# S5 matmuls on four 64x64 quadrants, the direct kernel's operand read in line, and the cell norm ahead of the output-gate blocks

## The chip, the core and the metric

The kernel runs on one core of a Trainium2 chip. The metric is the device time of one execution in microseconds (us). The engines are named as the profile names them: PE (TensorE's matmuls; PEld its weight loads), DVE (VectorE), ACT (ScalarE), POOL (GpSimd) and SP (SyncE, which issues most DMA transfers). Each engine works through its own list of instructions in order, and they meet through semaphores only.

## What is computed

One encoder layer on 272 positions (16 meta tokens and 256 inputs) of width 2048, in fp32:

```
z = RMSNorm(h) @ w_in                      # 2048 -> u_s5 1024 | qk 1024 | v 1024 | o 1024 | gates 32
y_s5: 64 groups of 16 channels, 64 complex states each, forward and backward:
    s[t] = lam * s[t-1] + Bbar u[t];  y = Re(C s) + d * u
    gelu, then y * sigmoid(y @ w_glu + b_glu), then RMSNorm
y_ml: mLSTM with 8 heads, forward and backward, num / max(|den|, exp(-m)), summed over both directions
    RMSNorm over each head's 128 values (the cell norm), times sigmoid(o)
h = h + [y_s5 || y_ml] @ w_out
h = h + (silu(conv(RMSNorm(h) @ w_gate)) * (RMSNorm(h) @ w_up)) @ w_down
out = RMSNorm(h)[16:]
```

## The kernel before, in words

Everything is held transposed: channels on the 128 partitions, positions along the free axis. `win_block(b)` (L455) makes one 128-row block of z: 16 matmuls of 128x128 weights (two records each in the trace, as every fp32 matmul), into a PSUM bank of the ring "mm". Block 0 is the gates, 1 to 8 are u, 9 to 16 q and k, 17 to 24 v, 25 to 32 o.

The S5 part cuts time into C = 68 chunks of T = 4 positions. A pair j of groups (32 pairs) has its first group on partitions 0 to 63 and its second on 64 to 127; m = 0 to 7 takes four pairs. The steps:

- `s5_tables` (L322) makes powers of lam from `par`, and `td`, a copy of some of them in DRAM.
- `in_coefs(m)` (L518) loads those (tcf) and builds the input coefficients on DVE (L529 to L532, ring of two). `in_proj(m)` (L535) multiplies them with U, the chunked input: per pair one bank of the ring "s5", eight 64x64 matmuls (L545), of which the first group uses rows and columns 0 to 63 of the array and the second rows and columns 64 to 127. ACT copies the bank to ST (L546).
- `rec_local`, `rec_carry`, `rec_spread` (L549 to L583) run the recurrence over chunks on DVE, in two halves of four m.
- `s5_coefs(m)` (L809) loads bc (512 KB, ring of two), builds zx and c1 on DVE (L822 to L832), and makes the direct kernel kp, the response within a chunk: per pair eight matmuls (L839) of 64 rows and 32 columns, each reading c1 as "k h", a stride of four elements, into the one bank "acc". Then come 32 matmuls mo (L856) of c1 with the states, into a bank of "s5". DVE adds d to the middle tap in PSUM (L863) and ACT copies kp to gx (L867, one buffer for two m). After each odd m, ACT issues four DMAs (L873) that spread gx into ms.
- `s5_out(b)` (L879), for the two m of b, is called after the s5_coefs that follows: POOL reorders ms to m0 (L881), PE adds m0 times U to the banks of mo (L887), ACT copies (L889), and two DMAs bring the result through `yd` back into U (L890, L891).
- `s5_gelu` (L898), later `s5_glu` (L908), which streams w_glu.

The mLSTM part: `gate_rows`, `qk_block`, `v_block`, `ml_meta`, then `ml_head(h)` for eight heads, with `den` kept in a bank "acc" over all of them and nb_ in "ml". `o_block(h)` makes the output gates. `ml_norm` (L764), a generator, takes 1/den, brings it through DRAM (rd) to all partitions as rb, scales num (L777 on DVE, L778 on POOL), squares it (L780), sums it on PE (L781), takes the root, and brings that through rsd to rsb for the products of L792 to L796. It runs after s5_glu. The products with w_out follow: first with the S5 half (L1030 on), where DVE multiplies each PSUM bank with R5 (t, L1042) and POOL adds it to h1, then with the mLSTM half (L1052 on). The MLP streams the rest.

Weights of mm3 and mm2 are split on the fly: `piece` loads raw (SP), ACT rounds to hi (L239), DVE makes lo (L240).

What sets the order: the code gives a program order and some pieces a high priority (`hp`). A planner of the framework (`schedule_with_timeline_sim=True`, L1149) then simulates the engines with its own costs, and puts on each engine what is ready in its simulation, by priority; that order is fixed in the program. `behind(a, b)` (L270) keeps a after b on one engine, without a wait. A ring's tile waits until the tile before it in the same buffer has been read. PSUM has eight banks: mm 2, s5 4, ml 1, acc 1 (L182).

## Time and profile before

| | |
|---|---|
| three runs | 1301.99 us median, 1300.67 to 1307.05 |
| profiled execution | 1304.81 us, its span 1303.0 us |
| mean granted TensorE clock | 0.983 |
| busy | PE 1238.1 us (95%), DVE 790.7 (61%), ACT 539.2 (41%), POOL 214.9 (16%) |
| chain that ended last, by engine | PE 76%, DVE 12%, DMA 7% |
| L466 (block matmuls), PE | 254.1 us |
| L266 and L267 (MLP), PE | 251.6 + 244.1 + 198.5 + 197.9 us |

The span is the time from the first to the last instruction of the profiled execution, and all stretches are in us from its start. A row of instructions gives engine, line, operation, output<-inputs and shape, and xcount; "idle before" is how long the engine stood before it, and the arrow names what ended that. The share of busy time is a mean over stages that have different limits; it says little about a single one.

### The profile page before, as it was taken

How to read it: one execution, taken by the hardware profiler on the slowest of the kernel's cores; microseconds unless marked ns; L12 is line 12 of the kernel's file. 1: busy time of each engine (PE TensorE's matmuls, PEld its weight loads, DVE VectorE, ACT ScalarE, POOL GpSimd, SP SyncE). 2: the span in 40 equal slices, each digit the busy share in tenths (PEclk: the TensorE clock that was granted, in tenths of full speed). 3: DMA queues.
4: the chain of work that ended last, by engine and by line, in shares of the span. 5: the costliest groups of instructions: out<-in, count | busy, mean ns of one | idle time of the engine just before them, and what ended most of it. 6: DMA issues, size and time to landing. Idle time of an engine off the chain costs nothing.

```text
span 1303.0 us, 21967 instructions
## 1 busy us (share of the span) xinstructions
PE 1238.1 (95%) x8865; PEld 1114.3 (86%) x8865; DVE 790.7 (61%) x1097; ACT 539.2 (41%) x858; POOL 214.9 (16%) x314
## 2 busy tenths in 40 slices
PE   6888998899999989999999999999999999999995
PEld 4777787778889879999999999888999999998885
DVE  4659998410114788766666665555666666665554
ACT  3522121232344545554444444333444444445552
POOL 1300000011210363221111111000111111120101
PEclk9989999999999999999999999999999999999998
DMA  9596433344325565555555556666555555556663
GB/s 340 146 274 188 149 130 107 93 148 146 109 62 177 168 208 164 181 187 182 186 183 183 188 183 180 192 192 190 187 188 182 187 184 182 189 173 194 188 193 113
DMA packets 88762, 227.79 MB, mean 175 GB/s; under 512 B 20604, under 2 KB 36436, under 8 KB 88660
## 3 DMA queue, kind: packets, MB, share of 16 engines
q1 hardware_dynamic: 81652, 223.95, 54.6%
q10 hardware_dynamic: 7008, 2.43, 0.7%
q8 instruction: 70, 1.15, 0.4%
q14 instruction: 32, 0.26, 0.1%
HBM read 219.81 MB, written 5.48 MB: 173 GB/s over the span
## 4 chain that ended last, share of the span: by engine, by line
PE 76%; DVE 12%; DMA 7%; issue 2%; ACT 1%; POOL 1%; ACTq 0%; SPq 0%; DVEq 0%; POOLq 0%
PE ps_mm L266 25%; PE ps_mm L267 13%; PE ps_mm L466 8%; PE ps_mm L255 8%; PE ps_mm L256 8%; PE ps_mm L257 8%; DMA bc<-bcs 1%; DVE ST L555 1%; DVE t L554 1%; DVE t L553 1%; DMA X<-xt 1%; DMA raw<-wglu 1%; DMA ms<-gx 1%; DVE ST L556 1%; DVE X L952 1%
## 5 line engine op out<-in xcount | busy, mean ns | idle before, releaser
L240 DVE TENSOR_TENSOR lo<-raw,hi 128x1024 fp32r<-128x1024 f32 (+1 forms) x312 | 392.9, 1259 | 256.7 <-ACT hi L239 230.2
L239 ACT ACTIVATE hi<-raw 128x1024 fp32r<-128x1024 f32 (+1 forms) x312 | 324.0, 1038 | 398.9 <-PE ps_mm L266 161.0
L466 PE MATMUL ps_mm<-X,wf 128*128 128x272 f32 (+1 forms) x1056 | 254.1, 400 | 19.1 <-DVE X L302 12.7
L466 PEld LDWEIGHTS ps_mm<-X,wf 128*128 128x128 f32 x1056 | 204.6, 196 | 61.3 <-DVE X L302 14.3
L266 PE MATMUL ps_mm<-X,hi 128*128 128x512 f32 x704 | 251.6, 398 | 0.0
L266 PE MATMUL ps_mm<-a,hi 128*128 128x512 f32 x704 | 244.1, 390 | 0.0
L256 PE MATMUL ps_mm<-X,hi 128*128 128x258 f32 x704 | 200.3, 284 | 0.0
L255 PE MATMUL ps_mm<-X,hi 128*128 128x258 f32 x704 | 198.9, 283 | 0.0
L267 PE MATMUL ps_mm<-a,lo 128*128 128x256 f32 x704 | 198.5, 282 | 0.0
L267 PE MATMUL ps_mm<-X,lo 128*128 128x256 f32 x704 | 197.9, 281 | 0.0
L257 PE MATMUL ps_mm<-X,lo 128*128 128x258 f32 x704 | 197.6, 281 | 0.0
L266 PEld LDWEIGHTS ps_mm<-X,hi 128*128 128x128 f32 x704 | 132.2, 188 | 30.2
L266 PEld LDWEIGHTS ps_mm<-a,hi 128*128 128x128 f32 x704 | 132.1, 188 | 27.7
L1094 POOL TENSOR_TENSOR gt<-gt,R 128x256 f32<-128x256 f32 x44 | 59.6, 1355 | 488.7 <-ACT gt L1093 488.7
L257 PEld LDWEIGHTS ps_mm<-X,lo 128*128 128x128 f32 x704 | 134.5, 191 | 0.0
L255 PEld LDWEIGHTS ps_mm<-X,hi 128*128 128x128 f32 x704 | 132.4, 188 | 1.9
L267 PEld LDWEIGHTS ps_mm<-X,lo 128*128 128x128 f32 x704 | 134.0, 190 | 0.0
L267 PEld LDWEIGHTS ps_mm<-a,lo 128*128 128x128 f32 x704 | 133.1, 189 | 0.0
L256 PEld LDWEIGHTS ps_mm<-X,hi 128*128 128x128 f32 x704 | 132.8, 189 | 0.0
L742 DVE SCALAR_TENSOR_TENSOR w<-ps_s,w 128x256 f32<-128x256 f32 (+3 forms) x32 | 10.2, 354 | 64.1 <-PE ps_s L730 42.1
L1099 DVE TENSOR_TENSOR u<-ps_mm,gt 128x512 f32<-128x512 f32 x44 | 30.4, 691 | 29.3 <-PE ps_mm L267 28.1
L255 PE MATMUL ps_mm<-y,hi 128*128 128x258 f32 x128 | 36.6, 288 | 6.5 <-DVE t L1042 5.9
(317 smaller groups left out, 1460.2 us busy)
## 6 DMA issues: line engine op xcount, KB each, us to landing
raw<-wg SPq DMA_DIRECT2D x88, 512.0 KB, 3.9
raw<-wu SPq DMA_DIRECT2D x88, 512.0 KB, 4.0
wf<-win SPq DMA_DIRECT2D x65, 512.0 KB, 4.0
raw<-wd SPq DMA_DIRECT2D x64, 512.0 KB, 3.6
raw<-wout SPq DMA_DIRECT2D x32, 512.0 KB, 4.1
raw<-wd SPq DMA_DIRECT2D x32, 384.0 KB, 3.8
tcf<-td SPq DMA_DIRECT2D x16, 256.0 KB, 7.1
bc<-bcs SPq DMA_DIRECT2D x8, 512.0 KB, 3.5
```

What stands on the lines that cost most here:

```text
L239: S.activation(hi[:, a:b], raw[:, a:b], AF.Copy)
L240: V.tensor_tensor(out=lo[:, a:b], in0=raw[:, a:b], in1=hi.bitcast(F32)[:, a:b], op=ALU.subtract)
L255: nc.tensor.matmul(out_ap, h, xh, start=(first and i == 0), stop=False)
L256: nc.tensor.matmul(out_ap, h, xl, start=False, stop=False)
L257: nc.tensor.matmul(out_ap, l, xh, start=False, stop=(last and i == n - 1))
L266: nc.tensor.matmul(both[:, :, :cols], h, x, start=(i == 0), stop=False)
L267: nc.tensor.matmul(both[:, 1, :cols], l, x[:, 0, :], start=False, stop=(i == n - 1))
L466: nc.tensor.matmul(p[:, :L - t0], w[k // 8][:, k % 8 * P:k % 8 * P + P], X[:, k, t0:], start=(k == 0), stop=(k == KD - 1))
L553: V.tensor_tensor(out=t1, in0=src, in1=lr[:, sl].unsqueeze(2).unsqueeze(3).to_broadcast([P, 32, 2, n]), op=ALU.mult)
L554: V.tensor_tensor(out=t2, in0=src[:, :, ::-1, :], in1=li[:, sl, :].unsqueeze(3).to_broadcast([P, 32, 2, n]), op=ALU.mult)
L1094: G.tensor_tensor(out=t, in0=t, in1=R2[:, 2:], op=ALU.mult)
L1099: V.tensor_tensor(out=u, in0=p.rearrange("p (j t) -> p j t", j=2), in1=t.unsqueeze(1).to_broadcast([P, 2, SEQ]), op=ALU.mult)
```

## The change

The inputs are laid out so that of every odd pair the two groups change places in the S5 parameters (`swapped` in `prepare`); U stays as it is. Matmuls of an even and an odd pair then take all four 64x64 quadrants in turn, into two banks (`rows_of(g ^ o)`). kp's columns lie as (h, k), so that c1 is read in line and the output goes in runs of four. kp takes two banks of "acc", which has two now; "ml" is gone and its users take "acc". The mo banks of an even and an odd pair serve two m. ACT copies kp before DVE adds d, in gx. POOL's copy in s5_out waits for the last mo of its two m. `par` is loaded behind the second X chunk instead of the last. ml_norm's first part (1/den) is emitted ahead of the o_blocks, its head loop behind them but ahead of s5_glu, its sums on PE behind the last o_block matmul; the rest stays behind s5_glu.

```diff
+    def swapped(a, ga, ja):
+        a = np.moveaxis(a, (ga, ja), (0, 1)).copy()
+        a[:, 1::2] = a[::-1, 1::2]
+        return np.moveaxis(a, (0, 1), (ga, ja))
+
     for i, a in enumerate((are, aim, ldt)):
         r = a.reshape(2, NP, 2, 64)
-        par[:, i, :64] = r.transpose(2, 3, 1, 0).reshape(P, 64)
+
+        par[:, i, :64] = swapped(r, 2, 1).transpose(2, 3, 1, 0).reshape(P, 64)
...
     def bank(tag):
-        return ps.tile([P, 512], F32, tag=tag, name="ps_" + tag, bufs={"mm": 2, "s5": 4, "ml": 1, "acc": 1}[tag])
+        return ps.tile([P, 512], F32, tag=tag, name="ps_" + tag, bufs={"mm": 2, "s5": 4, "acc": 2}[tag])
 
...
             behind(xd, last_raw[0])
             x_scale(q, a)
             if q == 1:
+                pd = nc.sync.dma_start(par, A["par"])
+                behind(pd, xd)
                 pieces.append(whole(w0[:, 1024:]))
-                behind(last_raw[0], xd)
-        pd = nc.sync.dma_start(par, A["par"])
-        behind(pd, xd)
+                behind(last_raw[0], pd)
+        pd = xd
     behind(nc.sync.dma_start(cst, A["cst"][:, :NC0]), pd)
     bts = [STf[:, 64 * C + 1024 * i:64 * C + 1024 * i + 1024] for i in range(4)]
...
+    def rows_of(g):
+        return slice(64 * g, 64 * g + 64)
...
     def in_proj(m, ic):
-        for q in range(4):
-            j = 4 * m + q
-            p = bank("s5")
-            pv = p[:, :4 * C - 4].rearrange("p (d r c) -> p d r c", d=2, r=2)
+        for q0 in (0, 2):
+            pv = [bank("s5")[:, :4 * C - 4].rearrange("p (d r c) -> p d r c", d=2, r=2) for _ in range(2)]
             for d in range(2):
-                uj = U[:, j, 0:C - 1] if d == 0 else U[:, j, UW - C + 1:][:, ::-1]
                 for ri in range(2):
-                    for g in range(2):
-                        gg = slice(64 * g, 64 * g + 64)
-                        nc.tensor.matmul(pv[gg, d, ri, :], ic[gg, q, d, ri, :], uj[gg], start=True, stop=True)
-            S.copy(ST[:, 2 * j:2 * j + 2, :, 1:], pv)
+                    for o in range(2):
+                        j = 4 * m + q0 + o
+                        uj = U[:, j, 0:C - 1] if d == 0 else U[:, j, UW - C + 1:][:, ::-1]
+                        for g in range(2):
+                            nc.tensor.matmul(pv[o][rows_of(g ^ o), d, ri, :], ic[rows_of(g), q0 + o, d, ri, :], uj[rows_of(g)],
+                                             start=True, stop=True)
+            for o in range(2):
+                j = 4 * m + q0 + o
+                S.copy(ST[:, 2 * j:2 * j + 2, :, 1:], pv[o])
 
...
         rd = dr.tile([40, N], F32, name="rd")
         nc.sync.dma_start(rd, rec)
         dump("rec", rec)
+        yield
...
-            nc.tensor.matmul(ss[:40, :N], er_(h), sq, start=(h == 0), stop=(h == 7))
+            behind(nc.tensor.matmul(ss[:40, :N], er_(h), sq, start=(h == 0), stop=(h == 7)), last_o[0])
             yield
...
+    pos = [None, None]
+    mo0, mo1 = {}, {}
+    gxs = [None]
+
     def s5_coefs(m, tb):
-        kp = bank("acc")
-        po = bank("s5")
-        mo0 = [None, None]
+        kp = [bank("acc"), bank("acc")]
+        if m % 2 == 0:
+            pos[:] = [bank("s5"), bank("s5")]
+            mo0.clear()
...
+        for i in range(2):
             for n_, (dd, ri) in enumerate(((1, 0), (1, 1), (0, 0), (0, 1))):
...
+                c0 = 0 if dd == 1 else 3
+                for o in range(2):
+                    w = (2 * (2 * i + o) + dd) * 2 + ri
+                    for g in range(2):
+                        gg = rows_of(g ^ o)
+                        mk_ = nc.tensor.matmul(
+                            kp[o][32 * g:32 * g + 32, 112 * i:112 * i + 112].rearrange("p (h k) -> p h k", k=7)[:, :, c0:c0 + 4],
+                            zx[gg, w].rearrange("p h e -> p (h e)"), c1[gg, w],
+                            start=(n_ == 0), stop=(n_ == 3), skip_group_check=True)
+                        if mkp is not None:
+                            behind(mk_, mkp)
+                        mkp = mk_
+        for i in range(2):
             for dd in range(2):
                 for ri in range(2):
...
+                    for o in range(2):
+                        j = 4 * m + 2 * i + o
+                        x = ST[:, 2 * j + dd, ri, 0:C]
+                        x = x if dd == 0 else x[:, ::-1]
+                        w = (2 * (2 * i + o) + dd) * 2 + ri
+                        cc_ = (2 * (m % 2) + i) * C
+                        for g in range(2):
+                            gg = rows_of(g ^ o)
+                            mo = nc.tensor.matmul(pos[o][rows_of(g), cc_:cc_ + C], c1[gg, w].rearrange("p h k -> p (h k)"), x[gg],
+                                                  start=((o, g) not in mo0), stop=False, skip_group_check=True)
+                            mo1[o] = mo
+                            if (o, g) not in mo0:
+                                mo0[o, g] = mo
+                            else:
+                                behind(mo, mo0[o, g])
         if m % 2 == 0:
             gxs[0] = gxr("gx", [P, 2, 4, 7, 16])[:64]
         gx = gxs[0]
...
+        for o in range(2):
+            S.copy(gx[:, m % 2, o::2], kp[o][:64, :224].rearrange("p (i h k) -> p i k h", i=2, k=7))
+        V.tensor_tensor(out=gx[:, m % 2, :, 3, :], in0=gx[:, m % 2, :, 3, :], in1=ed[:, 4 * m:4 * m + 4, :], op=ALU.add)
         if m % 2 == 0:
...
+            return None
 
         ms = m0r("ms", [P, 8, T, 16])
         for s in range(T):
             nc.scalar.dma_start(ms[s:P:T].rearrange("p e k h -> p e (k h)"),
                                 gx[0:64:2, :, :, 3 - s:7 - s].rearrange("p m q k h -> p (m q) (k h)"))
...
+        return ms
+
+    def s5_out(b, pos, ms, fence):
+        first = None
         m0 = m0r("m0", [P, 8, 16, T])
...
+        mc = G.tensor_copy(m0, ms.rearrange("p e k h -> p e h k"))
+
+        tc.add_manual_dep(mc.ins, fence.ins.name, mybir.DependencyInfo(
+            mybir.DependencyClass.Sync, mybir.DependencyReason.DATA), reason="bank")
         ysc = ysr("ysc", [P, 4, 2, C])
...
+        for i in range(2):
             for q in range(4):
+                cc_ = (2 * i + q // 2) * C
                 for g in range(2):
...
+                    gg = rows_of(g)
+                    mm_ = nc.tensor.matmul(pos[q % 2][gg, cc_:cc_ + C], m0[gg, 4 * i + q].rearrange("p h k -> p (h k)"),
+                                           U[gg, 8 * b + 4 * i + q, U0:U0 + C], start=False, stop=(i == 1 and q > 1), skip_group_check=True)
+                    if first is None:
+                        first = mm_
+                    else:
+                        behind(mm_, first)
+        for o in range(2):
+            S.copy(ysc[:, o::2].rearrange("p q m c -> p m q c"), pos[o][:, :4 * C].rearrange("p (m q c) -> p m q c", m=2, q=2))
         nc.scalar.dma_start(yd[b].rearrange("q x t m c -> (x t) q (m c)"), ysc.rearrange("p q m c -> p q (m c)"))
         nc.sync.dma_start(U[:, 8 * b:8 * b + 8, U0:U0 + C], yd[b].rearrange("q x t m c -> (q x) (t m) c"))
 
...
         ml_head(h)
+    nrm = ml_norm()
+    next(nrm)
     for h in range(8):
         o_block(h)
+    for h in range(8):
+        next(nrm)
     h1 = hx.tile([P, KD, N], F32, tag="h1", name="h1")
     o_gates()
     s5_glu()
-    for _ in ml_norm():
+    for _ in nrm:
         pass
```

## Rows read from the trace of the kernel before

**Rows 1.** busy us by stretch: length, PE, PEld, DVE, ACT, POOL, PEclk, DMA, GB/s

```profile
92.00:204.00 112.00, 102.03 (x716) 86.11 (x712) 108.73 (x209) 24.43 (x62) 1.08 (x15) 0.98 0.48 151
204.00:264.00 60.00, 51.07 (x1122) 47.82 (x1122) 33.73 (x46) 9.89 (x20) 4.63 (x3) 0.94 0.36 102
264.00:380.00 116.00, 114.14 (x579) 94.01 (x576) 14.60 (x42) 41.34 (x107) 21.38 (x43) 0.99 0.38 119
380.00:404.00 24.00, 24.00 (x116) 20.89 (x114) 2.45 (x2) 3.51 (x6) 0.00 (x0) 1.00 0.27 88
436.00:500.00 64.00, 54.76 (x400) 49.27 (x400) 49.07 (x61) 26.29 (x39) 36.93 (x32) 0.97 0.59 182
```

**Rows 2.** lines of PE, 204 to 273; behind the bar busy us, mean ns, idle

```profile
L839 PE MATMUL ps_acc<-c,zx 64*32 64x64 f32 x512 | 31.2, 291 | 6.8 <-DVE c L832 3.6 <-ACT gx L867 3.1
L856 PE MATMUL ps_s<-ST,c 64*64 64x68 f32 x512 | 16.9, 221 | 0.0
```

**Rows 3.** groups by line, PE, 60 to 130, the in-projection

```profile
L545 PE MATMUL ps_s<-U,ic 64*64 64x67 f32 x512 | 19.8, 242 | 8.0 <-DMA U<-ud 3.8 <-ACT ST L546 1.9 <-DVE ic L531 1.9
```

**Rows 4.** chain of waits, 204 to 275; start us, us, what

```profile
212.14 3.38 DMA bc<-bcs
...
227.84 4.87 DMA bc<-bcs
...
234.74 0.60 ACTq L873
...
241.15 1.84 POOL m L881
...
251.78 0.59 ACTq L873
...
264.70 0.04 ACT U L904
...
271.25 1.05 PE ps_s L887 x28
```

**Rows 5.** timeline of DVE, 90 to 275; start, us, instruction, count, idle, releaser

```profile
91.93 1.22 DVE L529 TENSOR_TENSOR ic<-tcf,ST 128x1024 f32<-128x1024 f32 x1 [1.73 <-PE ps_s L545]
...
210.89 1.23 DVE L830 TENSOR_TENSOR c<-bc,la 128x1024 f32<-128x1024 f32 x1 [0.44 <-PE ps_s L856]
...
240.86 1.23 DVE L831 TENSOR_TENSOR c<-bc,lb 128x1024 f32<-128x1024 f32 x1 [2.99 <-DMA bc<-bcs]
...
248.12 0.23 DVE L863 TENSOR_TENSOR ps_acc<-ps_acc,ed 64x64 f32<-64x64 f32 x1 [1.40 <-PE ps_acc L839]
...
250.09 1.22 DVE L830 TENSOR_TENSOR c<-bc,la 128x1024 f32<-128x1024 f32 x1 [1.16 <-PE ps_s L856]
...
251.35 1.22 DVE L832 TENSOR_TENSOR c<-c,c 128x1024 f32<-128x1024 f32 x1
```

**Rows 6.** timeline of PE, 196 to 276; the middle row from a window cut at 244.15

```profile
204.16 0.89 PE L839 MATMUL ps_acc<-c,zx 64*32 64x64 f32 x12 [3.61 <-DVE c L832]
...
244.13 0.28 PE L839 MATMUL ps_acc<-c,zx 64*32 64x64 f32 x2
...
264.08 5.31 PE L466 MATMUL ps_mm<-X,wf 128*128 128x272 f32 x22
```

**Rows 7.** groups by line, DVE, 436 to 500

```profile
L777 DVE TENSOR_TENSOR num<-num,rb 128x516 f32<-128x516 f32 x8 | 6.6, 830 | 5.2 <-DMA rb<-rd 5.2
L792 DVE TENSOR_TENSOR rsb<-num,rsb 128x258 f32<-128x258 f32 x8 | 5.6, 723 | 2.5 <-DMA rsb<-rsd 2.5
```

**Rows 8.** who waited for whom, PE, 436 to 500; total us, times, longest

```profile
PE ps_mm L255 <- DVE t L1042: 7.8, 5, 2.2
```

**Rows 9.** timeline of DVE, 0 to 40, one row

```profile
19.27 1.17 DVE L302 TENSOR_SCALAR X<-X,vec 128x272 f32<-128x272 f32 x4 [2.79 <-ACT sqx L300]
```

**Rows 10.** DMA packets, 8 to 22, while the inputs load

```profile
DMA packets 1658, 5.42 MB, mean 387 GB/s; under 512 B 184, under 2 KB 324, under 8 KB 1658
```

**Rows 11.** timeline of ACT, 196 to 276, the first ms issues

```profile
217.49 2.61 ACTq L873 DMA_DIRECT2D ms<-gx  x4
```

More of the change, by code (lines that the diff above doesn't have):

```diff
@@ L465, in win_block @@
         for k in range(KD):
-            nc.tensor.matmul(p[:, :L - t0], w[k // 8][:, k % 8 * P:k % 8 * P + P], X[:, k, t0:],
-                             start=(k == 0), stop=(k == KD - 1))
+            last_o[0] = nc.tensor.matmul(p[:, :L - t0], w[k // 8][:, k % 8 * P:k % 8 * P + P], X[:, k, t0:],
+                                         start=(k == 0), stop=(k == KD - 1))
         return p
@@ L620, in gate_rows @@
         for i in range(2):
-            pc = bank("ml")
+            pc = bank("acc")
             nc.tensor.matmul(pc[:, :40], c[:, META + 128 * i:META + 128 * i + 128], ident[:, :40], start=True, stop=True)
@@ L663, in v_block @@
             S.copy(vm[:, h, :], vt[:, 0:META])
-            pv = bank("ml")
+            pv = bank("acc")
             for i, src in enumerate((vt[:, 16:144], vt[:, 144:272])):
@@ L668, in v_block @@
             if h == 7:
-                pv = bank("ml")
+                pv = bank("acc")
                 nc.tensor.transpose(pv[:, :P], vm.rearrange("p h s -> p (h s)"), ident)
@@ L694, in ml_meta @@
             G.tensor_copy(kv[:, h // 2, h, :], (kE if h % 2 == 0 else kO)[:, h // 2, 0:16])
-        sm = bank("ml")
+        sm = bank("acc")
         for j in range(4):
@@ L745, in ml_head @@
         G.tensor_tensor(out=sm[:, 128:], in0=ab, in1=bb[:, 0:130], op=ALU.add)
-        nf, nb_ = bank("s5"), bank("ml")
+        nf, nb_ = bank("s5"), bank("acc")
         mmu = nc.tensor.matmul
@@ L832, in s5_coefs @@
         V.tensor_tensor(out=c1, in0=c1, in1=c2, op=ALU.add)
-        for qq in range(4):
+        for i in range(2):
             for n_, (dd, ri) in enumerate(((1, 0), (1, 1), (0, 0), (0, 1))):
-                c0 = 0 if dd == 1 else 48
-                w = (2 * qq + dd) * 2 + ri
-                for g in range(2):
-                    gg = slice(64 * g, 64 * g + 64)
-                    mk_ = nc.tensor.matmul(
-                        kp[32 * g:32 * g + 32, 112 * qq + c0:112 * qq + c0 + 64],
-                        zx[gg, w].rearrange("p h e -> p (h e)"),
-                        c1[gg, w].rearrange("p h k -> p k h"),
-                        start=(n_ == 0), stop=(n_ == 3), skip_group_check=True)
-                    if mkp is not None:
-                        behind(mk_, mkp)
-                    mkp = mk_
@@ L847, in s5_coefs @@
-        for qq in range(4):
-            j = 4 * m + qq
+                c0 = 0 if dd == 1 else 3
[10 more added lines that the diff above has]
+                        mkp = mk_
@@ L849, in s5_coefs @@
+        for i in range(2):
             for dd in range(2):
                 for ri in range(2):
-                    x = ST[:, 2 * j + dd, ri, 0:C]
-                    x = x if dd == 0 else x[:, ::-1]
-                    w = (2 * qq + dd) * 2 + ri
-                    for g in range(2):
-                        gg = slice(64 * g, 64 * g + 64)
-                        mo = nc.tensor.matmul(po[gg, qq * C:qq * C + C], c1[gg, w].rearrange("p h k -> p (h k)"), x[gg],
-                                              start=(mo0[g] is None), stop=False, skip_group_check=True)
-                        if mo0[g] is None:
-                            mo0[g] = mo
-                        else:
-                            behind(mo, mo0[g])
@@ L983, in body @@
     m0r = ring(lo_, "m0", 2)
-    pos, last = [], None
+    last = None
     for m in range(8):
-        po, m0 = s5_coefs(m, tb)
-        pos.append(po)
+        ms = s5_coefs(m, tb)
         if last is not None:
@@ L990, in body @@
             last = None
-        if m0 is not None:
-            last = (m // 2, pos, m0)
-            pos = []
+        if ms is not None:
+            last = (m // 2, list(pos), ms, mo1[1])
     s5_out(*last)
```

18 lines of the change are left out of this document (3 added, 15 removed).

## The prediction

> **What bounds the kernel now.** I read the busy shares by stage first [rows 1]. TensorE (PE) is busy 114.14 of 116 us from 264 on and 24.00 of 24 from 380 to 404: there whatever ends earlier ends the kernel earlier by as much. It is not the bound in three stretches: 92 to 204 us, where VectorE (DVE) is busy 108.73 of 112; 204 to 264, the S5 loop over m = 0 to 7; and 436 to 500, where PE sits idle 64.00 - 54.76 = 9.2 us. The change touches all three.
>
> Second, the groups of PE instructions in the S5 loop [rows 2] and in the in-projection [rows 3]. They are what the change rearranges: direct-kernel matmuls (L839) 31.2 us, state-to-output (L856) 16.9, in-projection (L545) 19.8. Each matmul is two records, so 512 records are 256 matmuls.
>
> Third, what ends the S5 loop, because its 51.07 busy PE microseconds of 60 make PE look like the bound. In the chain of waits [rows 4] the loop is something else. Up to 233 us it is a transfer of bc, 3.38 to 4.87 us, three times: bc has two buffers, so the load for m+2 is issued when L830 of m has read its buffer, and DVE, which works in order, then stands in L831 of m+2 until it lands (2.99 us the last time [rows 5]). From 234 us it is a round trip: ms transfers (issued by ACT), POOL's copy L881, PE's L887, yd, U, and then ACT's gelu L904, which stands in ACT's queue ahead of the next ms issues. The round that issues at 251.78 ends when gelu gets U at 264.70, the last ms issues follow it, and the last L887 starts at 271.25 [rows 4]. PE's kp and mo matmuls are in neither cycle.
>
> **The change part by part.**
>
> *In-projection on four quadrants.* Now two matmuls run side by side: a window cut at 244.15 us already holds two kp records, the first from 244.13 [rows 6], so they begin within 20 ns. 512 records in 19.8 us are 256 pairs of 77 ns; four side by side would halve that, 9.9 us. Nearly all of it lies under DVE's 108.73 of 112 us. What counts is when that stretch starts: L529 of m = 4 waited 1.73 us for L545 to free its coefficients [rows 5]. L545 for m = 1 and m = 2 both precede it, about 1 us saved in each, so that wait goes: -1.7 us. DVE, nearly without gaps up to the first kp matmul, which waited 3.61 us for DVE [rows 6], carries it on. What is late next is DVE itself. Bounds: 0 (ACT's copies hold the banks) and -2.0 (both halves in full).
>
> *kp and mo.* Four at once and the moving operand in line. kp now needs 31.2/256 = 122 ns a pair, mo 16.9/256 = 66 ns with four columns more; both read rows of 64 by 64. I put the difference on the stride of kp's read and take 66 ns for a group of four of either: 256 groups, 16.9 us instead of 48.1, so PE loses 31.2 us of work. In return kp's output is now written in runs of four; no row shows a strided write to PSUM. Its bounds are 66 ns (the same as mo) and 122 ns (as the strided read); I take 66, since the matmuls that already write whole rows differ from kp in the read alone. What is on the path of it: L830 of m = 2 waited 0.44 us for mo of m = 0 [rows 5], just ahead of the first bc issue: -0.4. The later waits of that kind, 1.40 us for kp and 1.16 for mo [rows 5], come while the gelu round runs and end nothing. So the 31.2 us do not reach the end by themselves; the loop keeps the pace of bc and of the round trip. Bounds for the loop: 0, and -31 if PE finds other work (below).
>
> *L863 after the copy.* Before, DVE added ed in PSUM, then ACT copied; now ACT copies both banks, one instruction more per m at 9.89/20 = 0.5 us [rows 1], and DVE adds in SBUF. The next kp waits for ACT alone. ACT is busy 9.89 of 60 us, so the eight extra copies are hidden; uncovered they would cost 4 us. The POOL copy L881 now also waits for the last mo of its pair. It waits for the ms transfers anyhow, which are issued later than that: nothing.
>
> *Cell norm ahead of the output-gate blocks.* Out of 436 to 500 go eight L777 (6.6 us, and the 5.2 us that DVE stood there for rb), with POOL's adds and ACT's squares; eight L792 (5.6 us, 2.5 us of waiting) stay [rows 7]. They go to 380 to 404, where DVE is busy 2.45 of 24 us and POOL not at all [rows 1]. PE's idle time at 436 to 500 is 7.8 us for DVE's t (L1042), queued behind those [rows 8]. Of the 11.8 + 8.1 us of DVE's queue that the norm takes there, 11.8 leave, 59%; of 9.2 us idle that is -5.5. Bounds 0 (the other half alone blocks as long) and -9.2. Its DMAs move too: the rd store and eight rb loads pass SP's queue ahead of the w_glu loads; PE has 24 us of block matmuls to cover them. The norm's eight sum matmuls are placed behind the last output block on PE and would wait there for ACT's squares if these came late; nothing taken.
>
> *par one place forward.* DVE stands 2.79 us before an X scaling [rows 9], which table work could fill (-2.8). Against that, 192 KB pass ahead of two X chunks. No row has that transfer alone; at the 387 GB/s of that stretch [rows 10] it is 0.5 us. The in-projection's start needs U, which doesn't hang on the tables: I take 0.
>
> *The ml bank becomes a second acc bank*: same eight banks. kp holds both, so a block-v transpose inside the loop queues with kp: 0, at most one copy's 0.5 us.
>
> **Sum.** -1.7 - 0.4 - 5.5 = -7.6 us on the profiled execution's 1304.81 (span 1303.0 and 1.8 around it), so 1297.2. That execution is 0.2% above the median of the three runs, 1301.99; from there 1294.4, call it 1294.
>
> A rule that speaks against four quadrants stands in the Trainium skill, "TensorE: Matmul & The Clock Gate", section "Wait — 56ns, not 53.3ns?": matmuls start no closer than about 25 ns apart however small they are. The trace disagrees inside a pair (two within 20 ns [rows 6]); no run here shows four. By the rule 1024 records of kp and mo would take 25.6 us, not 16.9; the sum doesn't hang on it, and the rival below in which PE fills the loop would be 1276 instead of 1269.
>
> **Rivals.**
>
> *The round trip loosens (20%), 1285.* The order on ACT and DVE is laid out by a planner, which sees other waits now. If ms of m = 7 is issued ahead of gelu: c of m = 7 is ready at 252.57 - 2.1 - 2.56 = 247.9 (L832's end, less the start's terms and the two waits of [rows 5]), kp, copies and add take about 2.2 us, first issue to POOL's end 8.2 (234.74 to 242.99), so the last L887 could start near 258 instead of 271.25 [rows 4, 5]. With the start's terms in it that is -13; I take -11, because the last transfer of the round before must be through, and -5.5 for the norm. For it: the gelu's place is one of order. Against: both depend on the same transfers as before.
>
> *PE fills the loop with block matmuls (18%), 1269.* If the planner knows that PE is free, it puts some 25 of the 31.2 us of v and output blocks in: -25 - 8 = -33. Against it: in the loop now no block matmul runs on PE from 205 until 264.08 [rows 6], though it idles 8.9 us: the planner took S5 for full, and counts as many matmuls as before.
>
> *DVE now waits for ACT (12%), 1309: slower.* Place: L863 in DVE's queue. It used to wait for PE; now for ACT's copy, which waits (gx has one buffer) until the ms transfers have read the pair before. From ACT's first ms issue to POOL's start it was 234.74 to 241.15, 6.4 us [rows 4], then about 0.8 for copies and add, then two coefficient builds of 5.6 us each (33.73 for six [rows 1]), each with a bc wait of some 3.4: 25 us a pair, against 17.3 now (217.49 to 234.74 [rows 4, 11]). Two pairs: +15.7, less 2.1 and 5.5, +8, and I take +7 since part of the build runs under the transfer. It decides as soon as ms lands later than L831 of the same pass ends: at 241.1 against 242.1 now, 1 us apart [rows 4, 5].
>
> *The quadrants don't run side by side, or strided writes cost as strided reads (8%), 1296.* The loop's pace hides most of that; the 1.7 us at the start is lost.
>
> **Numbers.** What can be told from no change here is about 0.5%, 6.5 us. The forecast as summed has 42%; its own range, from the bounds of norm, start and par, is 1287 to 1301. Below 1295.5 lie 0.26 of it, both middle rivals (0.38) and 0.03 of the last: faster 0.67. Same 0.16 + 0.05 = 0.21, slower 0.12. The range 1265 to 1304 leaves out part of the filled loop below and most of the slower case above.
>
> **What would show it.** L545, L839 and L856 each near half or less (9.9, 8.5, 8.5 us); four records begun within some 25 ns; the bc waits at L831 still there; gelu still ahead of the ms issues, the last L887 near 269; L1042 waits on PE under 4 us and L777 between 380 and 404. Wrong: block matmuls inside the S5 loop, a loop longer than 60 us with L863 waiting for ACT, or PE idle as before from 436 to 500.

## The result, and the profile after

The changed kernel takes 1286.61 us, the median of four runs (1282.82 to 1289.16), against 1302.39 us beside it: ratio 0.9871, 95% interval 0.9834 to 0.9907. Timed again it took 1284.79 us, ratio 0.9861 [0.9836, 0.9885]; the median of all nine runs is 1285.5, and the experiments are set against that. Forecast were 1294 and a range of 1265 to 1304. It is faster by twice what I summed, and just below the 1287 to 1301 us that the sum's own bounds gave. Its profiled execution took 1287.75 us, span 1286.0.

PE is busy 1204.7 us instead of 1238.1, so 33.4 us of its work are gone, but only 17.0 of the span: 16.4 us became idle time. Where, the windows of after say, columns as in [rows 1]:

```profile
0.00:92.00 92.00, 63.06 (x356) 49.97 (x357) 50.38 (x104) 33.09 (x97) 15.39 (x51) 0.91 0.80 252
92.00:204.00 112.00, 110.06 (x832) 90.81 (x830) 106.43 (x208) 25.27 (x68) 1.08 (x15) 1.00 0.52 164
204.00:264.00 60.00, 32.61 (x1141) 29.25 (x1141) 35.40 (x48) 9.66 (x27) 4.92 (x3) 0.77 0.41 117
272.00:404.00 132.00, 132.00 (x653) 108.54 (x653) 28.80 (x57) 46.78 (x117) 25.90 (x41) 0.99 0.45 135
436.00:500.00 64.00, 59.45 (x477) 58.85 (x477) 49.25 (x67) 29.04 (x42) 29.30 (x30) 0.97 0.56 181
```

In the S5 loop (204 to 264) PE's busy time falls from 51.07 to 32.61 us and the 60 us do not shrink. But from 92 to 204 PE is now full, 110.06 of 112, where it had 10 us of idle time [rows 1]. That is the row I had not foreseen. It must be read together with the row above it; in that stretch the kernel before had:

```profile
0.00:92.00 92.00, 71.39 (x436) 56.86 (x438) 50.92 (x105) 35.11 (x105) 17.34 (x51) 0.91 0.81 258
```

Up to 92 us PE is now busy 8.3 us less, so over the whole 204 us it idles as long as before (30.9 and 30.6 us). What changed is what it does in its busy time. The groups by line, answering [rows 2, 3]:

```profile
L862 PE MATMUL ps_acc<-c,zx 64*32 64x64 f32 x512 | 11.9, 255 | 6.1 <-DVE c L854 3.7 <-issue 2.4
L558 PE MATMUL ps_s<-U,ic 64*64 64x67 f32 x512 | 11.2, 235 | 7.9 <-ACT ST L562 6.8 <-DMA U<-ud 1.0
L880 PE MATMUL ps_s<-ST,c 64*64 64x68 f32 x512 | 11.2, 242 | 0.9 <-issue 0.9
L915 PE MATMUL ps_s<-U,m 64*64 64x68 f32 x128 | 8.3, 320 | 23.8 <-POOL m L905 23.8
```

The loop itself on PE's timeline, answering [rows 6] and the last line of [rows 4] (the bracket is the idle time before the row; the 245.85 x4 row is from a window cut at 245.872):

```profile
206.73 1.68 PE L862 MATMUL ps_acc<-c,zx 64*32 64x64 f32 x64 [2.62 <-DVE c L854]
...
240.95 2.08 PE L915 MATMUL ps_s<-U,m 64*64 64x68 f32 x32 [9.79 <-POOL m L905]
...
244.74 1.18 PE L880 MATMUL ps_s<-ST,c 64*64 64x68 f32 x64
...
245.85 1.10 PE L862 MATMUL ps_acc<-c,zx 64*32 64x64 f32 x64
...
245.85 0.26 PE L862 MATMUL ps_acc<-c,zx 64*32 64x64 f32 x4
...
269.09 2.08 PE L915 MATMUL ps_s<-U,m 64*64 64x68 f32 x32 [3.44 <-POOL m L905]
```

The loop starts 2.6 us later than before and its last output round 2.2 us earlier. What PE waits for is POOL's m, that is the ms transfers, 23.8 us in all. Behind such a wait it runs at the lower of its two clock levels, as the next windows show (the number behind the busy times is the granted clock, 0.50 for 1.2 GHz): output matmuls after 9.79 us of idle time take 2.08 us, where a round took 1.16 before, and kp matmuls of one m 1.93 us (first window) instead of 1.10 (third window).

```profile
224.57:226.40 1.83, 1.83 (x66) 1.69 (x64) 1.83 (x6) 0.57 (x2) 0.00 (x0) 0.50 0.15 46
240.95:243.03 2.08, 2.08 (x36) 1.95 (x40) 2.08 (x5) 0.18 (x1) 0.00 (x0) 0.50 0.03 8
244.75:247.00 2.25, 2.25 (x140) 2.09 (x138) 1.83 (x3) 0.58 (x2) 0.00 (x0) 1.00 0.33 96
```

ACT's timeline shows the round trip of [rows 4] twice more, and its end loosened: ms of the third pair is issued at 249.47 straight behind the gelu that got U at 249.40, but ms of the last pair at 259.74, ahead of its gelu.

```profile
249.40 0.43 ACT L937 ACTIVATE U<-U 128x272 f32<-128x272 f32 x1 [3.97 <-DMA U<-yd]
249.47 3.05 ACTq L898 DMA_DIRECT2D ms<-gx  x4
...
259.74 2.94 ACTq L898 DMA_DIRECT2D ms<-gx  x4
264.11 0.75 ACT L937 ACTIVATE U<-U 128x272 f32<-128x272 f32 x2 [4.70 <-DMA U<-yd]
```

Where the missing gain came from is seen in the block matmuls alone (L466 before, L475 after): busy time and records by stretch, first of before, then of after.

```profile
0.00:92.00 92.00, 61.21 (x224) 0.91 0.81 258
92.00:204.00 112.00, 90.73 (x396) 0.98 0.48 151
204.00:272.00 68.00, 5.31 (x22) 0.95 0.39 110
```

```profile
0.00:92.00 92.00, 58.10 (x220) 0.91 0.80 252
92.00:204.00 112.00, 103.09 (x448) 1.00 0.52 164
204.00:272.00 68.00, 5.38 (x21) 0.77 0.41 120
```

161.19 us of blocks are done by 204 instead of 151.94: 9.25 us more, with the loop's end no later and as many blocks in the loop. PE did this in the same busy time because the in-projection took 11.2 us instead of 19.8. Behind the loop PE has no gaps to 404, so this work is simply missing there. Last, the stretch from the first matmul of the gated unit (`s5_glu`) to the first of the MLP, of before and of after:

```profile
403.80:540.70 136.90, 126.56 (x980) 120.39 (x979) 106.28 (x130) 73.14 (x118) 58.00 (x53) 0.99 0.60 189
```

```profile
396.60:523.60 127.00, 121.02 (x967) 118.95 (x967) 96.70 (x119) 67.18 (x106) 45.09 (x45) 0.99 0.57 185
```

It is 9.9 us shorter. Part of that only moved: of the norm's sum matmuls (L798, 16 records) 12 now run just ahead of it, and all 16 (L781) ran inside it before.

```profile
393.85 2.80 PE L798 MATMUL ps_acc<-hsq,er 128*40 128x258 f32 x12
```

So the norm is worth 9.9 - 2.8 = 7.1 us; PE's idle time in the stretch fell by 4.4 us (10.3 to 6.0). The sum by position: start of the last output round 2.2 us earlier, from there to the gated unit 5.1 us less (-9.25 for the blocks, +2.8 for the sum matmuls, and some +1.4, of which about 0.9 is the last output round at the lower clock), the stretch 9.9 us less: together -17.2 against -17.0 of the spans. What follows, from the MLP on, takes 762.3 us in both.

### The profile page after: what moved, and what is told of

Its sections match the earlier page's. It is cut to its first block, busy times and chain, and to the rows that moved or that the text cites. A ratio compares the mean times of both kernels' runs of the same rounds, so it can differ in the third digit from the quotient of the medians.

```text
span 1286.0 us, 21964 instructions
## 1 busy us (share of the span) xinstructions
PE 1204.7 (94%) x8865; PEld 1082.6 (84%) x8865; DVE 789.6 (61%) x1097; ACT 535.2 (42%) x864; POOL 208.7 (16%) x314
## 4 chain that ended last, share of the span: by engine, by line
PE 76%; DVE 2%; DMA 1%; issue 0%; ACT 0%; ACTq 0%; POOL 0%; DVEq 0%; POOLq 0%; SPq 0%
PE ps_mm L274 25%; PE ps_mm L275 13%; PE ps_mm L264 9%; PE ps_mm L263 9%; PE ps_mm L265 8%; PE ps_mm L475 7%; PE ps_s L746 1%; DMA rsb<-rsd 1%; PE ps_s L264 1%; PE ps_s L263 1%; PE ps_s L265 1%; DMA ms<-gx 0%; PE ps_s L764 0%; DVE h L1167 0%; PE ps_acc L767 0%
## 5 line engine op out<-in xcount | busy, mean ns | idle before, releaser
L475 PE MATMUL ps_mm<-X,wf 128*128 128x272 f32 (+1 forms) x1056 | 253.2, 399 | 23.0 <-DVE X L310 10.9
L475 PEld LDWEIGHTS ps_mm<-X,wf 128*128 128x128 f32 x1056 | 203.5, 195 | 64.1 <-DVE X L310 18.0
```

The lines of the kernel that those rows point to most:

```text
L475: last_o[0] = nc.tensor.matmul(p[:, :L - t0], w[k // 8][:, k % 8 * P:k % 8 * P + P], X[:, k, t0:], start=(k == 0), stop=(k == KD - 1))
```

## The experiments

My theory after the two traces: the gain is the block matmuls ahead of the loop (through the in-projection), the norm, and a little of the loop; kp's and mo's 25 us do not reach the end. The rival: PE's savings in the loop are what counts.

**The norm's part undone.**

```
-        yield
...
-            behind(nc.tensor.matmul(ss[:40, :N], er_(h), sq, start=(h == 0), stop=(h == 7)), last_o[0])
+            nc.tensor.matmul(ss[:40, :N], er_(h), sq, start=(h == 0), stop=(h == 7))
...
-    nrm = ml_norm()
-    next(nrm)
     for h in range(8):
         o_block(h)
-    for h in range(8):
-        next(nrm)
...
-    for _ in nrm:
+    for _ in ml_norm():
         pass
```

> The changed kernel with one part undone: the cell norm's per-head work stands behind the output-gate blocks and the gated unit again; everything ahead of it keeps its order. If the norm's move pays through PE's wait for DVE's t (my step of 5.5 us; the two traces show PE's idle time between 436 and 500 us as 9.2 before and 4.55 after): 4 to 5.5 us slower than the changed kernel, with 8 to 10 us of PE idle time in the 64 us ahead of 500, named as waits for t. Rival, that the half of the norm that stays blocks DVE's queue as long and that the idle time fell because all stages shifted: within 1 us of the changed kernel.

1290.43 us, ratio to before 0.9904 [0.9884, 0.9924]: 4.9 us slower than the changed kernel, as the first theory had it. The same stretch (gated unit to MLP) lasts 135.40 us, first row, against 128.00 in the second execution of the changed kernel, second row. Of these 7.4 us, 2.8 are again sum matmuls that run ahead of it there; the other 4.6 are what the times show. The wait for t, though, is not where I expected the whole of it: over the stretch PE waits 6.0 us for t here, against 5.4 in the first profile of the changed kernel and 2.9 in the second (which has a wait of 2.1 us for ACT's hi instead), and from 436 to 500 PE idles 64.00 - 58.69 = 5.3 us, not 8 to 10. The idle time of the two rows differs by 7.55 - 5.64 = 1.9 us; the rest I cannot put to a single wait.

```profile
389.10:524.50 135.40, 127.85 (x981) 121.66 (x980) 107.05 (x130) 72.34 (x117) 56.64 (x53) 0.97 0.60 191
```

```profile
392.70:520.70 128.00, 122.36 (x968) 120.54 (x968) 96.83 (x119) 67.07 (x106) 44.99 (x45) 0.97 0.56 184
```

**The in-projection two side by side.**

```
-            for d in range(2):
-                for ri in range(2):
-                    for o in range(2):
+            for o in range(2):
+                for d in range(2):
+                    for ri in range(2):
```

> The changed kernel with the in-projection's matmuls two side by side again (the even pair's eight, then the odd pair's eight); kp, mo, norm and par as changed. The planner now lays 313 block matmuls on PE ahead of the first kp instead of 333 (the kernel before: 310). If the missed gain is the in-projection's time, turned into 20 to 23 block matmuls ahead of the S5 loop: 20 x 0.48 us = 8 to 10 us slower than the changed kernel, the in-projection's group at 19 to 22 us instead of 11.2, and the first kp no later than in the changed kernel (206.7). Rival, my own prediction, that all but a wait of 1.7 us of it lies under DVE's work: 0 to 2 us slower. Second rival, that the extra blocks were room which the planner had anyway: within 1 us.

1293.62 us, 0.9926 [0.9910, 0.9942]: 8.1 us slower. That is the first theory's 8 to 10; my prediction's 0 to 2 us is refuted. The block matmuls by 204 us are back to 57.23 + 96.10 = 153.3 us (the group of L475 in this kernel), the first kp is at 207.04 and the last output round starts at 267.53, so the loop is not what it lost.

```profile
207.04 1.65 PE L862 MATMUL ps_acc<-c,zx 64*32 64x64 f32 x64 [2.12 <-DVE c L854]
...
267.53 1.16 PE L915 MATMUL ps_s<-U,m 64*64 64x68 f32 x32 [0.17 <-POOL m L905]
```

```profile
0.00:92.00 92.00, 57.23 (x215) 0.91 0.77 250
92.00:204.00 112.00, 96.10 (x410) 0.97 0.48 151
```

```profile
92.00:204.00 112.00, 104.83 (x794) 87.70 (x793) 106.04 (x207) 24.78 (x66) 1.08 (x15) 0.97 0.48 151
```

```profile
L558 PE MATMUL ps_s<-U,ic 64*64 64x67 f32 x512 | 14.0, 237 | 8.7 <-ACT ST L562 6.2 <-DVE ST L594 2.5
```

The last two rows hold a second surprise. The group takes 14.0 us and not the 19 to 22 expected, so on the chip the four quadrants save only 2.8 us against this order, yet the blocks lose 8 us: PE idles 7.2 of the 112 us instead of 1.9, and 35.5 us instead of 30.9 up to 204. The planner, which lays the order out with costs of its own, puts 313 block matmuls ahead of the first kp here and 333 in the changed kernel. The pairs' saving of 5.8 us against the kernel before thus mostly became idle time, the quadrants' saving became blocks. That the planner puts more blocks in only when the in-projection looks short to it is an inference; no run shows its costs.

**par behind the X chunks again.**

```
             if q == 1:
-                pd = nc.sync.dma_start(par, A["par"])
...
+        pd = nc.sync.dma_start(par, A["par"])
+        behind(pd, xd)
```

> The changed kernel with the load of par behind all X chunks again. The order on ACT and DVE between 55 and 95 us goes back with it to that of the kernel before (gate rows ahead of the first coefficients); block matmuls ahead of the loop stay 333. If par's move is what made the gate rows late, so that ACT's exp of pm stood 10.1 us ahead of the copies of ST and the first kp came at 206.7 instead of 204.2: the first kp at 202 to 204.5, and 2.5 to 4.5 us faster than the changed kernel. Rival, my prediction of 0 for par: within 1 us. Rival, that table work fills DVE's early wait (2.8 us) and that it reaches the end: 2.8 us slower.

1284.09 us, 0.9859 [0.9837, 0.9880]: 1.4 us faster than the changed kernel, inside the scatter. The 2.5 to 4.5 us of the main case did not come. The first kp does come at 203.43, 3.3 us earlier, but the last output round starts at 269.19 against 269.09: the loop takes it back. By this, par's move is worth nothing that can be told at the end, as predicted, though not at the loop's start.

**kp and mo two side by side; kp's strided read; both together.**

```
-            for n_, (dd, ri) in enumerate(((1, 0), (1, 1), (0, 0), (0, 1))):
-                c0 = 0 if dd == 1 else 3
-                for o in range(2):
+            for o in range(2):
+                for n_, (dd, ri) in enumerate(((1, 0), (1, 1), (0, 0), (0, 1))):
+                    c0 = 0 if dd == 1 else 3
...
-            for dd in range(2):
-                for ri in range(2):
-                    for o in range(2):
+            for o in range(2):
+                for dd in range(2):
+                    for ri in range(2):
```

```
-                c0 = 0 if dd == 1 else 3
+                c0 = 0 if dd == 1 else 48
...
-                            kp[o][32 * g:32 * g + 32, 112 * i:112 * i + 112].rearrange("p (h k) -> p h k", k=7)[:, :, c0:c0 + 4],
-                            zx[gg, w].rearrange("p h e -> p (h e)"), c1[gg, w],
+                            kp[o][32 * g:32 * g + 32, 112 * i + c0:112 * i + c0 + 64],
+                            zx[gg, w].rearrange("p h e -> p (h e)"), c1[gg, w].rearrange("p h k -> p k h"),
...
-            S.copy(gx[:, m % 2, o::2], kp[o][:64, :224].rearrange("p (i h k) -> p i k h", i=2, k=7))
+            S.copy(gx[:, m % 2, o::2], kp[o][:64, :224].rearrange("p (i k h) -> p i k h", i=2, k=7))
```

> The changed kernel with kp and mo two side by side again (even pair's matmuls, then odd pair's), the read of the moving operand still in line. If the S5 loop keeps the pace of bc and of the round trip (my step): kp and mo take 10 to 24 us more of PE's time between them, and the kernel stays within 2 us of the changed one. Rival, that PE's saving in the loop is what reaches the end: 8 to 14 us slower. By the groups this also splits kp's and mo's price: at 66 ns a pair each of them is 16.9 us, and what kp has over that is the strided write.

> The changed kernel with kp's moving operand read with a stride again and its output written in whole rows of 64; four quadrants as changed. If the stride of the read is what made a kp pair 122 ns (my step), a group of four now takes near 115 ns at full clock: kp for one m 1.9 us instead of 1.10, the group near 16 to 18 us instead of 11.9, and the time stays within 2 us since the loop hides it. Rival, that the price was that of two against four side by side: kp stays at 1.1 to 1.2 us for one m.

> The changed kernel with both parts of kp's and mo's change undone together: strided read and whole rows written for kp, two side by side for both; the order on PE is that of the changed kernel. Half of it alone cost nothing that can be told (two side by side: 1286.1 us; strided read: 1287.3; changed: 1284.8 and 1286.6). If the loop's pace is bc's and the round trip's (my step): kp and mo take over 35 us of PE's time instead of 23 and the kernel stays within 2.5 us of the changed one, 1283 to 1288. Rival, that the 3 to 5 us which the norm's and the in-projection's undoing leave unexplained of the gain are the loop's, and come only when PE gets back to nearly full in it: 1288 to 1291, with a last output round of 3 to 5 us later than in the changed kernel.

Two side by side 1286.10 us, 0.9867 [0.9849, 0.9884]; strided read 1287.25, 0.9880 [0.9856, 0.9903] of two runs; both 1285.65, 0.9862 [0.9844, 0.9879]. The groups by line, kp and mo of the first, kp of the second, kp and mo of the third:

```profile
L862 PE MATMUL ps_acc<-c,zx 64*32 64x64 f32 x512 | 15.1, 255 | 7.9 <-DVE c L854 6.2 <-issue 1.7
L880 PE MATMUL ps_s<-ST,c 64*64 64x68 f32 x512 | 15.1, 249 | 0.0
```

```profile
L862 PE MATMUL ps_acc<-c,zx 64*32 64x64 f32 x512 | 17.1, 291 | 7.8 <-DVE c L854 6.0 <-issue 1.7
```

```profile
L862 PE MATMUL ps_acc<-c,zx 64*32 64x64 f32 x512 | 20.9, 293 | 4.9 <-DVE c L854 4.9
L880 PE MATMUL ps_s<-ST,c 64*64 64x68 f32 x512 | 13.7, 233 | 0.0
```

Two side by side cost 7.1 us more of PE's time, not the 10 to 24 expected: in this order a pair takes less than the 66 ns of before. The third kernel has 11.5 us more, and is 0.2 us from the changed one. So at least 11.5 of the 25.0 us that kp and mo lost are hidden. The rest is not undone here: no run has the order of the kernel before, in which all pairs use the same two quadrants, with its 31.2 and 16.9 us. The rival's last output round 3 to 5 us later did not come either (270.47), but PE is busy only 39.49 of the 60 us in that run, so a PE "nearly full" again, as the rival wants it, was not tried.

By the second, 16 groups of four with the strided read take 2.04 to 2.06 us on its timeline, 128 to 129 ns each, against 69 with the read in line: the price is the read's. Writing PSUM in runs of four costs nothing that shows: 69 ns for a group of kp, 74 for one of mo, which writes whole rows and four columns more.

```profile
246.25 2.06 PE L862 MATMUL ps_acc<-c,zx 64*32 64x64 f32 x64
...
250.22 2.04 PE L862 MATMUL ps_acc<-c,zx 64*32 64x64 f32 x64
```

**The gate rows behind the in-projection; the gelus behind the last ms issue.** The changed kernel once more ran beside these two:

> The changed kernel itself, timed beside the next three so that differences of 2 to 4 us can be read: 1284 to 1290 us by its earlier times (1282.8 to 1289.2). If its trace repeats the first, the first kp starts within 0.5 us of 206.7 and the last matmul of the direct kernel's output near 269 to 271 us.

1284.79 us. Its first kp starts at 207.97, not within 0.5 us of 206.73, and its last output round at 268.18 instead of 269.09, so a difference of about 1 us between single traces says nothing. In the first edit `st_cp` holds the last coefficient instruction and the last copy of ST of m = 3.

```
+        gr[0] = V.tensor_tensor(out=cM[:, 1:2], in0=cM[:, 1:2], in1=kc("mcol"), op=ALU.add)
+        behind(gr[0], st_cp[0])
...
-        S.activation(pm[:, 1:N], nb[:, 1:N], AF.Exp, bias=cM[:, 0:1])
+        behind(S.activation(pm[:, 1:N], nb[:, 1:N], AF.Exp, bias=cM[:, 0:1]), st_cp[1])
```

> The changed kernel with par's new place kept, and three instructions of the gate rows put behind in their engines' queues: the two exps of pm on ACT behind the last copy of ST of m = 3, and the add of cM on DVE behind the coefficients of m = 3. Nothing is left out. If the late start of the S5 loop comes from these standing ahead (ACT stood 10.1 us for nb, PE then 6.8 us for the copies of ST, DVE 5.2 us for PE and 9.2 us for cM): the first kp 3 to 8 us earlier than 206.7, and the kernel 2 to 5 us faster than the changed one, as with par put back. Rival, that U's arrival ends that stretch and the wait moves to DMA tcf or U: first kp within 1 us, time within 1.5 us. Second rival, that the loop takes the gain back (with par put back its first kp was 3.3 us earlier and its last output matmul started at 269.2 against 269.1): first kp earlier, the loop's end within 1 us, and the time falls only by what block matmuls PE then runs earlier, 0 to 2 us.

```
-        S.activation(g, g, AF.Gelu_apprx_tanh)
+        behind(S.activation(g, g, AF.Gelu_apprx_tanh), ms_last[0])
```

> The changed kernel with all gelus behind the last ms issue on ACT's queue. In the trace of the changed kernel ms of the third pair is issued at 249.47, straight behind a gelu that got U at 249.40, though its gx was ready at 245.7; the pair after it follows that round. If the gelu's place is what ends the loop: the last round of m0 starts 3.5 to 4.5 us earlier than 269.1, and the kernel is 3 to 4.5 us faster, as all PE work behind it moves up. Rival, that the bc transfers (waits of 2 to 2.7 us in each pass) and the single gx buffer set the pace: under 1.5 us earlier, time within 1.5 us. Second rival, that the gelus then come late for the gated unit: PE waits for them after 400 us, 1 to 3 us slower.

1283.24 us, 0.9843 [0.9819, 0.9866], and 1282.62 us, 0.9834 [0.9816, 0.9851], beside 1284.79: 1.5 and 2.2 us, less than each theory's main case and not told from nothing by themselves. In the traces they act where they should: the first kp at 204.44 and the last output round at 264.40 with the gate rows behind; that round at 266.09, though the first kp is at 208.53, with the gelus behind. The edit put only the first of the two exps behind; the second now waits on ACT for the add of cM that was moved, ahead of eight copies of ST (from 90.52), so this run does not show what the gate rows are worth as a whole:

```profile
89.37 0.29 ACT L726 ACTIVATE pm<-nb,cM 128x1 f32<-128x1 f32 x1 [10.73 <-DVE cM L649]
```

What the gate rows did in the changed kernel is on ACT, then PE, then DVE (three timelines):

```profile
78.45 0.51 ACT L720 ACTIVATE pm<-nb,cM 128x257 f32<-128x257 f32 x1 [10.14 <-DMA nb<-nmm]
```

```profile
80.34 2.33 PE L558 MATMUL ps_s<-U,ic 64*64 64x67 f32 x64 [6.80 <-ACT ST L562]
```

```profile
82.72 1.23 DVE L538 TENSOR_TENSOR ic<-tcf,ST 128x1024 f32<-128x1024 f32 x1 [5.23 <-PE ps_s L558]
...
94.44 1.23 DVE L538 TENSOR_TENSOR ic<-tcf,ST 128x1024 f32<-128x1024 f32 x1 [2.18 <-PE ps_s L558]
```

ACT stands for nb with the copies of ST queued behind it, PE waits for a bank, DVE for the coefficients' buffer. The wait of [rows 5] that I let go at 91.93 is here again at 94.44.

**The loop's idle time filled with output-gate blocks, then with v blocks.** The first moves one output-gate block ahead of the loop and four into it, the second the last five v blocks in the same way, with transposes in the mm banks. What goes into the loop stays between mo and the output matmuls. In both, the q and k blocks and the first three v blocks are also emitted ahead of the loop, where most of them ran anyway (336 block matmuls stand ahead of the first kp, 333 in the changed kernel). The first edit, where `om` yields the blocks' matmuls, each kept behind the last mo, and `last_o` is the last of them:

```
+        for _ in range((16, 24, 16, 8)[b]):
+            next(om)
         first = None
         m0 = m0r("m0", [P, 8, 16, T])
...
                     if first is None:
                         first = mm_
+                        behind(mm_, last_o[0])
```

> The changed kernel with five output-gate blocks moved: one ahead of the S5 loop and 64 matmuls of four others between mo and the direct kernel's output matmuls inside it, fenced so that they stay there; the first three v blocks are emitted ahead of the loop. Nothing is left out. PE idles 27.4 us from 204 to 264 us of the changed kernel, and is busy without a gap from 272 to 404. If PE's whole sequence is what ends the kernel and the loop's idle time is free: 64 x 0.46 us = 29 us of blocks go in, the loop gets up to 8 us longer since they exceed some of the gaps, and the clock no longer falls in it: 18 to 25 us faster than the changed kernel, near 1265. Rival, that the loop's own chain (gelu, U, ms, bc) grows by as much as is put in: within 4 us of the changed kernel. Second rival, that the blocks taken from 300 to 404 uncover the norm's and the gated unit's loads there: gain in the loop as above, but 5 to 10 us of new idle time from 380 to 440.

> The changed kernel with v blocks in place of output-gate blocks in the S5 loop: the last five v blocks are taken from behind the loop, one ahead of it and 64 block matmuls inside it, their transposes in the mm banks; all eight output-gate blocks stay behind the loop. Nothing is left out. The run with output-gate blocks in the loop gained 1.5 us only, with 8.3 us of new PE idle time for the norm's squares between 380 and 440. If that came from taking away the blocks that cover heads and norm: here PE is busy in the loop as there (near 51 of 60 us), the idle time at the norm does not come, and the kernel is 15 to 22 us faster than the changed one (1263 to 1270). Rival, that heads and norm have a chain of their own that starts only with the loop's end and lasts as long however little PE has to do: the stretch from the loop's end to the first out-projection stays as long as it was, within 5 us, PE idles in it instead, and the kernel gains under 4 us.

> The v blocks in the loop, with the gate rows behind the in-projection and all gelus behind the last ms issue as in the two runs before. If the three act in different places: 3 to 5 us below the run with v blocks alone. Rival, that with PE filled the loop is PE's, so that a faster ms round gives nothing: within 1.5 us of it.

Output-gate blocks: 1283.34 us, 0.9841 [0.9821, 0.9860], 1.5 us from the run beside it, which is not told from nothing, and far from the 18 to 25 us of the main case. The loop was filled (busy 50.99 of 60) and its last output round started 2.8 us later (271.91), but PE then stood in the norm, from which the cover had been taken, that is the independent work that hides a wait: second row, 8.3 us idle of 24, and the wait by name.

```profile
204.00:264.00 60.00, 50.99 (x1137) 43.87 (x1139) 38.02 (x49) 12.28 (x31) 3.88 (x3) 0.97 0.54 166
...
380.00:404.00 24.00, 15.73 (x84) 10.01 (x82) 12.29 (x15) 8.47 (x18) 6.89 (x8) 0.74 0.58 177
```

```profile
PE ps_acc L798 <- ACT hsq L797: 8.3, 6, 5.2
```

v blocks: 1266.70 us, 0.9717 [0.9696, 0.9739]; with the gate rows and the gelus behind as well 1263.76, 0.9705 [0.9689, 0.9721]. PE is busy about as long in the loop, and the stretch after it has its cover:

```profile
204.00:264.00 60.00, 49.39 (x1122) 40.86 (x1120) 35.59 (x47) 11.63 (x36) 3.53 (x3) 0.94 0.54 163
264.00:372.00 108.00, 106.26 (x652) 88.76 (x651) 26.70 (x56) 43.45 (x113) 29.44 (x51) 0.98 0.44 125
```

So the loop's idle time was worth some 19 us, as expected (15 to 22), to whoever fills it with work that nothing else needs as cover. The kernel with all three is the fastest here, 21.7 us below the changed kernel; what the last two edits add to the v blocks, 2.9 us, lies between the two expectations and is again within the scatter.

## Why the prediction was right, and which terms were not

- The bound. That "the loop keeps the pace of bc and of the round trip" held as far as it was tried: 48.1 us of kp and mo became 23.1, and undoing 11.5 of them moved nothing that can be told. The bc waits at L853 are still there (1.98, 2.17, 2.23 and 2.72 us).
- The price of a group. 66 ns were forecast; at the upper clock level 16 groups of kp take 1.10 us, 69 ns, and of mo 1.18 us, 74 ns, so the step was right. At that pace the sums would be 8.8 and 9.4 us. They are 11.9 and 11.2 instead of the 8.5 forecast for each, mostly because PE, now often idle in the loop, runs part of them at the lower level (kp of one m 1.93 us at a granted clock of 0.50). I priced the groups at the clock of before.
- The loop's ends. -2.1 was forecast, -2.2 came, by another way, so that agreement is luck. The start did not come 1.7 us earlier but 2.6 later, since L538's wait did not go (2.18 at 94.44). The loop itself, first kp to last output round, is 62.4 us instead of 67.1: the last ms issue went ahead of its gelu. That is the rival "the round trip loosens" in its place, with a part of its 13 us. That the rounds before still have gelu ahead is a likely reason for the rest: with all gelus behind the last issue the loop took 57.6 us (208.53 to 266.09).
- The mis-sized term: the in-projection. "Nearly all of it lies under DVE's 108.73 of 112 us", so the step had only the wait of 1.7 us. DVE is as busy as that, but the 8.5 us that PE no longer spends on the in-projection did not become idle time: 9.25 us of block matmuls stand in their place, and undoing this edit alone costs 8.1 us. The step took a stage in which DVE is the busiest for one in which PE's time is worth nothing, though PE had block matmuls to run there that it otherwise runs behind the loop, where it is the bound. The rival "PE fills the loop with block matmuls" had the mechanism and looked for it in the wrong stage; I had argued that the planner took the loop for full, and did not ask what it does ahead of the loop.
- The norm. -5.5 was forecast; undoing it costs 4.9 us, and the two profiles give 7.1. L794 did move ahead (the last four from 380.0 to 383.3). L1077's waits fell from 7.8 to 5.4 us in one trace and to 2.9 in the other, so "under 4 us" holds in one of two, and the run with the norm undone has 6.0 and not 7.8. The size is about right; that it comes through this wait is shown only in part.
- ACT ahead of DVE, the slower rival: L892 waits for ACT 6.24 and 4.20 us, late in the loop, where no coefficients follow on DVE. The place was right, the price nil.
- The quadrants do run side by side, so that rival is gone. par: nothing that can be told at the end, as taken. The ml bank was put back in no run.

The central value was 8 us too high mainly for one reason, the 9.25 us of blocks. The time fell into the range of 1265 to 1304 because the range was drawn for the rivals too; the sum's own bounds end just above it.

Open remains how the rest of the gain divides: undoing the norm and the in-projection's quadrants brings back 4.9 and 8.1 of the 16.9 us, and no run undoes the loop's 2.2 us, nor the whole of kp, mo and in-projection. Open are also why the norm's part is larger than its waits, and whether the blocks could stand ahead of the loop with pairs alone, which no kernel here forced.

## What to carry to other kernels

Time saved on the engine that bounds the whole counts wherever that engine has independent work to pull forward, even in a stage where another engine is the busiest: when an edit frees it, ask what the planner will put in that place. Its idle time is free room in the same way, not only in the stage one edits. But work that fills one gap may be the cover of another: moved output-gate blocks gained nothing that can be told (1.5 us), moved v blocks 19. And a queue in order makes neighbours pay: one exp standing for a DMA held up three engines for 5 to 10 us each, and what was got back by moving it and one add, 1.5 us, is within the scatter.

## What the hardware showed that was not expected

- Four small matmul records on four quadrants begin within 22 ns (the x4 row cut at 245.872), and sixteen such groups take 1.10 to 1.18 us, 69 to 74 ns each. The Trainium skill, "TensorE: Matmul & The Clock Gate", section "Wait — 56ns, not 53.3ns?", has a floor of about 25 ns between starts; for tiles on different quadrants this trace does not show it.
- With a strided moving operand a group of four takes 128 to 129 ns against 69 with the read in line. A strided pair took 122 ns before [rows 2], and 78 (first row below, 2.48 us for 32) where consecutive runs of matmuls change quadrants. The strided groups take as long at either clock level: in the run with the strided read, one m took 2.06 us at 246.25, where the granted clock was 0.50, and 2.04 at 250.22, where it was 1.00.
- Pairs alone are faster when consecutive runs of eight matmuls change quadrants: mo took 1.59 us for one m in the kernel with pairs (second row below), 50 ns a pair, against 66 before [rows 2], at the same count and size. There the bank changes with the quadrants. In the in-projection, where the bank changes from run to run in both kernels, 128 records took 3.11 us with the change of quadrants and 3.95 before, both at a granted clock of 1.00, so the bank is not the reason there.

```profile
250.25 2.48 PE L862 MATMUL ps_acc<-c,zx 64*32 64x64 f32 x64
```

```profile
216.80 1.59 PE L880 MATMUL ps_s<-ST,c 64*64 64x68 f32 x64
```

- Less PE work made the rest of it slower: with the loop half empty an output round took 2.08 instead of 1.16 us, and the filled loop brought it back (4.7 us for all four with output-gate blocks in it, against 8.3).
